# Seven products of quarters in chunks 6 to 10 of the first feed-forward, and the S5 tables and the memory norm moved into chunks 1 to 5

## The chip, the cores and the metric

The kernel runs on one core of a Trainium2 chip. Its time is the device time of one execution in microseconds (us), the median of several runs. All matrices are float32. TensorE (PE) multiplies and transposes into PSUM; VectorE (DVE), ScalarE (ACT) and GpSimd (POOL) work on SBUF, the first two on PSUM too; SyncE (SP) issues most of the DMAs.

## The reference, cut to what matters

```
h = x
h = h + 0.5 * swiglu(rmsnorm(h, g_ffn1), w1_gate, w1_up, w1_down)     # first feed-forward
u = rmsnorm(h, g_mix) @ w_in                                           # mixer: S5 scan and pooling
h = h + concat(rmsnorm(s5(u[:, :1024])), rmsnorm(pool(u[:, 1024:]))) @ w_out
h = h + cross_attention(rmsnorm(h, g_xattn), rmsnorm(mem, g_mem))
h = h + 0.5 * swiglu(rmsnorm(h, g_ffn2), w2_gate, w2_up, w2_down)     # second feed-forward
return rmsnorm(h, g_final)
swiglu(x, g, u, d) = (silu(x @ g) * (x @ u)) @ d
```

There are 256 tokens, the model width is 2048, the hidden width of a feed-forward 5632. The S5 tables (powers of the discretised state matrix, and products of them with B and C) and the norm of the memory depend on no activation, so they can be worked out at any time before the mixer and the attention.

## The kernel before

Each float32 operand is split into a high and a low part (`fp32r`), and a product is three matmuls: high by high, high by low, low by high. A weight tile has 128 x 4 x 512 numbers (1 MB). SyncE loads it into one of three `raw` buffers (pool `wraw`), ScalarE copies a half of it to `whi` (L142), VectorE subtracts that from the half to get `wlo` (L143), and PE uses a half in 12 matmuls of 512 columns: two blocks, two groups of 128 tokens (`lt`), three matmuls (L156 to L158). The activations are the stationary operand, the weights move. A tile is 24 matmuls.

A feed-forward goes over the hidden width in 11 chunks of 512. In a plain chunk the gate needs four weight tiles and the up product four, 192 matmuls in all; `gated` (L274) and `upped` (L285) form the product of the two, `act_tiles` (L289) transposes it (8 matmuls of 128 columns), and four more tiles (96 matmuls) multiply it by the down weights; `add_to_h` (L261) adds the accumulators to `h`. A pass is a group of chunks whose down products are accumulated together.

The first feed-forward (`ffn`, L297) runs plain chunks in the passes `PASSES` of 3, 3, 3 and 2 chunks; the down products of a pass follow its last chunk. The accumulators lie in `psA`, 6 banks, 2 for a gate and 2 for an up product. `begin` (L560) is chunk 0: it loads x, splits it, fills `h` by transposes and takes the gate and up products of a tile pair in turn, with four accumulators open at once. Only behind it does `ffn_norm` (L269) work out the norm of x from the sums of squares that `squares` collects, and `gated` needs its result `hcol`. A generator, `aside` (L544), holds the S5 tables (`s5_tables`, L345) and then the memory norm; `step` (L302) takes a step of it at 5 of 9 tiles, from the seventh on, over the whole feed-forward. Its tiles lie in the pool `pp`.

The second feed-forward is written out of its own (L1020 on). Its passes, `PASSES2`, have two chunks each and one at the end. `psA` has 4 banks for gates and ups and 2 more, `dacc`, for the down products of the pass before, which are taken in steps between the products of the next chunks. Chunks 0 and 1 are plain, chunks 2 to 10 are `seven` (L1100): tokens, inputs and outputs of the upper half of the inputs are taken as quarters, and seven products of 12 matmuls stand for eight; the lower half is plain (`eight`, four tiles). That is 84 + 96 = 180 matmuls in place of 192, for 8 more subtractions of 128 x 1024 (`less`, L1064), and sums of accumulators. `token_sums` (L1083) forms the four sums of token quarters, SH and SL, in two buffers of `wraw`. The halves of weights lie in five pairs of buffers in turn, `pairs[:] = [whl, sw, whl, sw, whl]` (L1079): three in the pool `whl`, two in the pool `sw`. In the first feed-forward there are the three of `whl` alone.

Tile pools are closed and opened in the order of the program; a planner orders the instructions of each engine by program order and by its own costs, and the instructions named in `keep_in_program_order` keep their place.

Of the kernel before, what the change touches and what calls it, by code (L numbers as in the profile page):

```python
# [14 lines left out]
P = 128  # L15
# [8 lines left out]
PASSES2 = ((0, 2), (2, 4), (4, 6), (6, 8), (8, 10), (10, 11))  # L24
PASSES = ((0, 3), (3, 6), (6, 9), (9, 11))
# [29 lines left out]
def block_kernel(ctx: ExitStack, tc: tile.TileContext, xT, memT, wgu1, wd1, w_in, w_glu, w_pool, w_out,  # L55
# [10 lines left out]
    banks = ExitStack()  # L66
    psA = banks.enter_context(tc.tile_pool(name="psA", bufs=6, space=bass.MemoryType.PSUM))
    psB = banks.enter_context(tc.tile_pool(name="psB", bufs=2, space=bass.MemoryType.PSUM))
# [228 lines left out]
    def ffn(fe, wgu, wd, xs, aside=None, begin=None, before=None, after=None):  # L297


        calls = [0]  # L300

        def step():  # L302
            calls[0] += 1
            if aside is not None and calls[0] > 6 and calls[0] * 5 % 9 < 5:
                next(aside, None)

        late = []

        def held(more=None):
            def run(i):  # L310
                if i == 0:
                    while late:
                        late.pop(0)()
                if more is not None:
                    more(i)
                step()
            return run

        for a, b in PASSES:
            acts = []  # L320
            for f in range(a, b):
                if f == 0 and begin is not None:
                    ag, au = begin()
                else:
                    ag, au = tok_unit([cols4(wgu[4 * f:4 * f + 4, 0], i) for i in range(4)], xs, held(before if f == 0 else None)), None
                if f == 0:
                    ffn_norm()
                ss = gated(fe, ag)
                if au is None:
                    au = tok_unit([cols4(wgu[4 * f:4 * f + 4, 1], i) for i in range(4)], xs, held())  # L330
                upped(ss, au)
                late += [lambda ss=ss, t=t: act_tiles(ss, acts, t) for t in range(2)]
            for n in range(ND):
                more = None
                if b == FC and after is not None:
                    more = lambda i, n=n: after(n, i)
                add_to_h(tok_unit([cols4(wd[f, 4 * n:4 * n + 4], 0) for f in range(a, b)], acts, held(more)), n, qcol)
                if b == FC:
                    squares(n)
        if aside is not None:  # L340
            for _ in aside:
                pass

# [199 lines left out]
    with tc.tile_pool(name="pp", bufs=1) as pp, tc.tile_pool(name="fe1", bufs=2) as fe:  # L543
        def aside():  # L544
            yield from s5_tables(pp)
            ss = pp.tile([P, L], F32, name="ssm")
            mt_ = {}
            for k in range(KT + 4):
                if k < KT:
                    mt_[k] = pp.tile([P, L], F32, name="mem", bufs=6)  # L550
                    tc.keep_in_program_order(V.memset(mt_[k][:, :1], 0.0))
                    G.dma_start(out=mt_[k], in_=memT[:, k])
                if k > 3:
                    square_into(ss, mt_[k - 4], k == 4, pin=True)
                if k % 2 == 0:
                    yield
            rnorm(ss, D, rmcol)
            spread(rmcol, Rm)

        def begin():  # L560
# [64 lines left out]
        ffn(fe, wgu1, wd1, xs, aside(), begin,  # L625
            after=lambda n, i: layer_in(xm, n - 1, G_MIX, [xp] * KT) if n > 0 and i == 1 else None)
# [393 lines left out]
    banks.close()  # L1020
    psA = ctx.enter_context(tc.tile_pool(name="psC", bufs=4, space=bass.MemoryType.PSUM))
    psB = ctx.enter_context(tc.tile_pool(name="psD", bufs=2, space=bass.MemoryType.PSUM))
    fe = ctx.enter_context(tc.tile_pool(name="fe2", bufs=2))
    gate_up = lambda f, m: wgu2[4 * f:4 * f + 4, m]
    late = []

    def flush(n=2):
        for _ in range(min(n, len(late))):
            late.pop(0)()

    def finish_chunk(ss, acts):
        late.extend([lambda t=t: act_tiles(ss, acts, t) for t in range(2)])

    def plain(f, acts, before=None):
        def first(i):
            flush()
            if before is not None:
                before(i)

        ag = tok_unit([cols4(gate_up(f, 0), i) for i in range(4)], xf, first)  # L1040
        if f == 0:
            ffn_norm()
        ss = gated(fe, ag, 2)
        upped(ss, tok_unit([cols4(gate_up(f, 1), i) for i in range(4)], xf))
        finish_chunk(ss, acts)

    def down(a, b, acts, accs_of=tok_accs, done=None):

        for n in range(ND):
            accs = accs_of()  # L1050
            for i, f in enumerate(range(a, b)):
                blocks = wtile(cols4(wd2[f, 4 * n:4 * n + 4], 0))
                flush()
                for j, w in enumerate(blocks):
                    tok_block(accs, w, acts[4 * i + j], i + j == 0, f == b - 1 and j == 3)
                if f == b - 1:
                    add_to_h(accs, n, qcol)
                    if done is not None:
                        done(n)
                yield  # L1060

    def less(out, a, b):
        for c in (0, 256):
            V.tensor_tensor(out=out[:, :, c:c + 256], in0=a[:, :, c:c + 256], in1=b[:, :, c:c + 256], op=ALU.subtract)  # L1064

    def product(acc, w, x, first, last):

        acc = acc.rearrange("p (f c) -> p f c", f=4)
        for j, (wh, wl) in enumerate(parts(w)):
            xh, xl = x(j)  # L1070
            T.matmul(acc, xh, wh, start=first and j == 0, stop=False)  # L1071
            T.matmul(acc, xh, wl, start=False, stop=False)  # L1072
            T.matmul(acc, xl, wh, start=False, stop=last and j == 3)  # L1073

    def quarter(k, lt):
        return lambda j: [xf[k + j][:, i * L + lt * P:i * L + (lt + 1) * P] for i in range(2)]

    with tc.tile_pool(name="sw", bufs=1) as sw:
        pairs[:] = [whl, sw, whl, sw, whl]  # L1079
        SH = sw.tile([P, 4, 4, P], F32R, name="SH")  # L1080
        SL = sw.tile([P, 4, 4, P], F32R, name="SL")

        def token_sums():  # L1083

            x = wraw.tile([P, 8, L], F32, name="raw")
            for k in range(8):
                V.tensor_tensor(out=x[:, k], in0=xf[k][:, :L].bitcast(F32), in1=xf[k][:, L:].bitcast(F32), op=ALU.add)
            q = [[x[:, 4 * i:4 * i + 4, lt * P:(lt + 1) * P] for i in range(2)] for lt in range(2)]
            s = wraw.tile([P, 4, 4, P], F32, name="raw")
            for o, a, b, op in ((0, q[1][0], q[1][1], ALU.add), (1, s[:, 0], q[0][0], ALU.subtract),  # L1090
                                (2, q[0][0], q[1][0], ALU.subtract), (3, q[0][1], s[:, 1], ALU.subtract)):
                V.tensor_tensor(out=s[:, o], in0=a, in1=b, op=op)
            for o in (0, 2):
                S.activation(out=SH[:, o:o + 2], in_=s[:, o:o + 2], func=AF.Copy)
                V.tensor_tensor(out=SL[:, o:o + 2], in0=s[:, o:o + 2], in1=SH[:, o:o + 2].bitcast(F32), op=ALU.subtract)

        def tsum(o):
            return lambda j: (SH[:, o, j], SL[:, o, j])

        def seven(f, acts, steps):  # L1100

            g, u = gate_up(f, 0), gate_up(f, 1)
            
            def step():
                flush()
                next(steps, None)


            def load(pool, name, src):
                r = pool.tile([P, 4, 512], F32, name=name)  # L1110
                src(r)
                return r

            tmp = lambda: psB.tile([P, 512], F32, name="psb")
            s1, s5, u2, u3 = (sw.tile([P, 512], F32, name=n) for n in ("s1", "s5", "u2", "u3"))
            t = sw.tile([P, 4, 512], F32, name="t")
            gate, up = ([psA.tile([P, 512], F32, name="acc") for _ in range(2)] for _ in range(2))
            eight = lambda accs, w, i: [tok_block(accs, b, xf[4 * i + j], i == 2 and j == 0, i == 3 and j == 3)
                                        for j, b in enumerate(wtile(cols4(w, i)))]
            r11 = load(wraw, "raw", cols4(g, 0))  # L1120
# [41 lines left out]
        for a, b in PASSES2:  # L1162
            acts = []
            for f in range(a, b):
                if f < 2:
                    plain(f, acts, (lambda i: layer_in(xf, ND - 1, G_FFN2, [xp] * KT) if i == 3 else None) if f == 0 else None)
                    if f == 0:
                        token_sums()
# [129 lines left out]
```

## Time and profile before

| | us |
|---|---|
| median of 3 runs (2132.37 to 2134.86) | 2133.53 |
| the profiled execution | 2133.47 |
| its span, first to last instruction | 2131.7 |
| PE busy / DVE / ACT / POOL | 2094.1 / 1502.4 / 1076.6 / 142.7 |
| mean granted clock of PE | 0.995 |

The page of the profile gives the busy time of each engine, the chain of work that ended last, and the costliest groups of instructions. A line that begins with `L142 ACT` is a group: line of the kernel, engine, operation, output and inputs. In a timeline each line is a start, a duration, an engine, a line and an operation. PE is the weight-streaming engine, PEld its loading of the stationary operand.

### The profile page before, as it was taken

Reading aid. Unit: us, or ns where it says so; the run is one execution under the profiler, and the core shown is the slowest. Engines: PE = TensorE matmul, PEld = TensorE weight load, DVE = VectorE, ACT = ScalarE, POOL = GpSimd, SP = SyncE. Lnnn points to the kernel's source line nnn. Section 1 sums busy time; section 2 is a strip of 40 time slices with the busy share of each in tenths; the row PEclk is TensorE's granted clock in tenths of the full one; section 3 lists DMA queues with packets and bytes.
Section 4 is the critical chain, followed back from the end, with each engine's and each line's share of the span. In section 5 each row is a group of like instructions: output and inputs, shape, how many; then the busy total and the mean of one; then the engine's idle time right before and its main releaser. Section 6 shows DMA issues by size and latency. Waiting matters only on the chain.

```text
span 2131.7 us, 26764 instructions
## 1 busy us (share of the span) xinstructions
PE 2094.1 (98%) x10248; PEld 1730.5 (81%) x10248; DVE 1502.4 (70%) x2021; ACT 1076.6 (51%) x1505; POOL 142.7 (7%) x255
## 2 busy tenths in 40 slices
PE   8999999999999999979999999999999999999997
PEld 7888888888888888867888888888888888888885
DVE  5567766666655667836867755566888888888875
ACT  6543444344444555635665644545555555555543
POOL 0000011111110001850000000000000000000000
PEclk9999999999999999999999999999999999999998
DMA  7756777777766657768544546557565666565542
GB/s 243 209 183 197 206 214 223 218 218 219 229 212 195 226 191 238 252 204 254 197 162 176 202 173 220 195 172 224 177 199 178 195 208 210 180 199 191 178 157 99
DMA packets 202464, 427.58 MB, mean 201 GB/s; under 512 B 17888, under 2 KB 31392, under 8 KB 193248
## 3 DMA queue, kind: packets, MB, share of 16 engines
q1 hardware_dynamic: 180992, 391.75, 58.1%
q0 software_dynamic: 6416, 18.85, 3.0%
q10 hardware_dynamic: 14928, 15.28, 2.3%
q8 instruction: 80, 1.31, 0.2%
q14 instruction: 48, 0.39, 0.1%
HBM read 408.05 MB, written 16.78 MB: 199 GB/s over the span
## 4 chain that ended last, share of the span: by engine, by line
PE 94%; POOL 3%; DMA 1%; DVE 1%; ACT 1%; issue 0%; DVEq 0%; ACTq 0%; SPq 0%
PE acc L158 19%; PE acc L157 19%; PE acc L156 19%; PE acc L120 7%; PE acc L121 4%; PE dacc L156 3%; PE dacc L157 3%; PE dacc L158 3%; PE psb L1072 2%; PE psb L1073 2%; PE psb L1071 2%; PE acc L998 1%; PE acc L999 1%; PE acc L997 1%; PE acc L1072 1%; PE acc L1071 1%
## 5 line engine op out<-in xcount | busy, mean ns | idle before, releaser
L143 DVE TENSOR_TENSOR wlo<-raw,whi 128x1024 fp32r<-128x1024 f32 x522 | 635.9, 1223 | 357.1 <-ACT whi L142 354.9
L142 ACT ACTIVATE whi<-raw 128x1024 fp32r<-128x1024 f32 x522 | 553.0, 1060 | 641.7 <-PE acc L158 461.1
L157 PE MATMUL acc<-wlo,x 128*128 128x512 f32 x1760 | 689.9, 392 | 0.0
L158 PE MATMUL acc<-whi,x 128*128 128x512 f32 x1760 | 687.6, 392 | 0.0
L156 PE MATMUL acc<-whi,x 128*128 128x512 f32 x1760 | 638.5, 393 | 8.2 <-ACT x L191 7.9
L156 PEld LDWEIGHTS acc<-whi,x 128*128 128x128 f32 x1760 | 330.6, 188 | 78.6 <-ACT x L191 7.9
L158 PEld LDWEIGHTS acc<-whi,x 128*128 128x128 f32 x1760 | 330.9, 188 | 70.7 <-issue 1.2
L157 PEld LDWEIGHTS acc<-wlo,x 128*128 128x128 f32 x1760 | 331.0, 188 | 70.0 <-issue 0.6
L120 PE MATMUL acc<-x,whi 128*128 128x512 f32 x848 | 299.7, 399 | 2.4 <-ACT whi L100 2.4
L101 DVE TENSOR_TENSOR wlo<-raw,whi 128x1024 fp32r<-128x1024 f32 (+1 forms) x144 | 172.1, 1199 | 133.6 <-ACT whi L100 133.0
L121 PE MATMUL acc<-x,wlo 128*128 128x256 f32 x848 | 234.9, 283 | 0.9 <-DVE wlo L101 0.8
L100 ACT ACTIVATE whi<-raw 128x1024 fp32r<-128x1024 f32 (+1 forms) x144 | 147.0, 1024 | 163.0 <-PE acc L120 99.3
L120 PEld LDWEIGHTS acc<-x,whi 128*128 128x128 f32 x848 | 158.4, 188 | 40.8 <-ACT whi L100 4.2
L121 PEld LDWEIGHTS acc<-x,wlo 128*128 128x128 f32 x848 | 159.0, 189 | 5.3 <-DVE wlo L101 2.5
L156 PE MATMUL dacc<-whi,x 128*128 128x512 f32 x320 | 124.9, 395 | 1.0 <-DVE h L267 1.0
L158 PE MATMUL dacc<-whi,x 128*128 128x512 f32 x320 | 125.7, 393 | 0.0
L157 PE MATMUL dacc<-wlo,x 128*128 128x512 f32 x320 | 125.4, 392 | 0.0
L142 ACT ACTIVATE whi<-t 128x1024 fp32r<-128x1024 f32 x54 | 57.4, 1062 | 50.4 <-PE acc L158 30.2
L143 DVE TENSOR_TENSOR wlo<-t,whi 128x1024 fp32r<-128x1024 f32 x54 | 65.0, 1224 | 20.5 <-ACT whi L142 19.6
L143 DVE TENSOR_TENSOR wlo<-r,whi 128x1024 fp32r<-128x1024 f32 x54 | 65.9, 1220 | 15.2 <-ACT whi L142 15.2
L142 ACT ACTIVATE whi<-r 128x1024 fp32r<-128x1024 f32 x54 | 56.3, 1059 | 36.6 <-PE acc L158 15.1
L156 PEld LDWEIGHTS dacc<-whi,x 128*128 128x128 f32 x320 | 60.1, 188 | 14.2 <-issue 1.3
(287 smaller groups left out, 2132.2 us busy)
## 6 DMA issues: line engine op xcount, KB each, us to landing
raw<-in_wgu SPq DMA_DIRECT2D x148, 1024.0 KB, 6.1
raw<-in_wd SPq DMA_DIRECT2D x88, 1024.0 KB, 5.3
r<-in_wgu SPq DMA_DIRECT2D x27, 1024.0 KB, 6.1
raw<-in_w_in SPq DMA_DIRECT2D x16, 1024.0 KB, 5.0
raw<-in_w_k SPq DMA_DIRECT2D x16, 1024.0 KB, 5.0
raw<-in_w_out SPq DMA_DIRECT2D x32, 512.0 KB, 5.1
raw<-in_w_q SPq DMA_DIRECT2D x16, 1024.0 KB, 4.8
raw<-in_w_v SPq DMA_DIRECT2D x16, 1024.0 KB, 4.8
```

Source lines behind the costliest of these rows:

```text
L100: S.activation(out=hi[:, :n], in_=r, func=AF.Copy)
L101: V.tensor_tensor(out=lo[:, :n], in0=r, in1=hi[:, :n].bitcast(F32), op=ALU.subtract)
L120: T.matmul(acc, w[0], x, start=first, stop=False)
L121: T.matmul(acc[:, :L], w[1], x[:, :L], start=False, stop=last)
L142: S.activation(out=hi, in_=raw[:, :, c:c + 256], func=AF.Copy)
L143: V.tensor_tensor(out=lo, in0=raw[:, :, c:c + 256], in1=hi.bitcast(F32), op=ALU.subtract)
L156: T.matmul(acc, xh, w[0], start=first, stop=False)
L157: T.matmul(acc, xh, w[1], start=False, stop=False)
L158: T.matmul(acc, xl, w[0], start=False, stop=last)
L1071: T.matmul(acc, xh, wh, start=first and j == 0, stop=False)
L1072: T.matmul(acc, xh, wl, start=False, stop=False)
L1073: T.matmul(acc, xl, wh, start=False, stop=last and j == 3)
```

## The change

`ffn` now serves both feed-forwards, with the passes of two chunks for both and with the chunk from which `seven` is used: 6 in the first, 2 in the second. The first feed-forward therefore has 4 + 2 accumulator banks in place of 6 (`open_banks`), takes its down products between those of the next chunks, and opens the pool `sw` at chunk 6, in the room of `pp`, which must be done by then. The generator `aside` begins with the memory norm, then makes the tables, and takes 1 or 2 steps in turn at each of the 8 gate and up tiles of chunks 1 to 5. `token_sums` is called ahead of chunk 5 (first) and of chunk 1 (second feed-forward). `pairs` has `sw` only from the first chunk with seven products on, which in the second feed-forward is chunk 2, no longer chunk 0. In the last chunk, two steps of the down products are taken at each of four places, where there was one.

```diff
-PASSES = ((0, 3), (3, 6), (6, 9), (9, 11))
+PASSES = ((0, 2), (2, 4), (4, 6), (6, 8), (8, 10), (10, 11))
+SEVEN1 = 6
+SEVEN2 = 2
...
-    psA = banks.enter_context(tc.tile_pool(name="psA", bufs=6, space=bass.MemoryType.PSUM))
+    def open_banks(n):
+        banks.close()
+        return [banks.enter_context(tc.tile_pool(name="ps", bufs=b, space=bass.MemoryType.PSUM)) for b in (n, 2)]
+
+    psA, psB = open_banks(4)
...
+        def steps(slot, slots=4):
+            flush()
+            for _ in range((slot + 1) * todo[1] // slots - slot * todo[1] // slots):
+                next(todo[0], None)
+
+        def plain(f):
+            def ahead(m):
+                def run(i):
+                    if i % 2 == 1 or todo[1] == 0:
+                        steps(2 * m + i // 2)
+                    if before is not None and f == 0 and m == 0:
+                        before(i)
+                    if tick is not None:
+                        tick()
+                return run
...
         for a, b in PASSES:
             acts = []
             for f in range(a, b):
+                if f == seven_from - 1:
+                    SH, SL = (fe.tile([P, 4, 4, P], F32R, name=n, bufs=1) for n in ("SH", "SL"))
+                    token_sums()
+                if f == seven_from:
+                    sw = room()
+                    pairs[:] = [whl, sw, whl, sw, whl]
+                ss = seven(f) if f >= seven_from else plain(f)
...
+            if b < FC:
+                todo[0] = down(wd, a, b, acts, lambda: [psA.tile([P, 512], F32, name="dacc", bufs=2) for _ in range(2)])
+                n = next(y - x for x, y in PASSES if x == b)
+                todo[1] = ND * (b - a) // n
+        pairs[:] = [whl]
+        return down(wd, *PASSES[-1], acts, done=squares if done is None else done)
...
-            yield from s5_tables(pp)
             ss = pp.tile([P, L], F32, name="ssm")
...
             spread(rmcol, Rm)
+            yield from s5_tables(pp)
...
+        def tick():
+            count[0] += 1
+            for _ in range(1 + (count[0] % 2)):
+                next(side, None)
+
+        def room():
+            for _ in side:
+                pass
+            spare.close()
+            return spare.enter_context(tc.tile_pool(name="sw", bufs=1))
+
+        for n, i in ffn(fe, wgu1, wd1, xs, SEVEN1, room, begin, tick=tick):
+            if n > 0 and i == 0:
+                layer_in(xm, n - 1, G_MIX, [xp] * KT)
+        spare.close()
+    psA, psB = open_banks(6)
```

`seven`, `token_sums`, `product`, `less` and `down` are those of the second feed-forward before, moved up.

## Rows read from the trace of the kernel before

**Rows 1.** The page: busy time of the engines, and the chain by engine.
```profile
PE 2094.1 (98%) x10248; PEld 1730.5 (81%) x10248; DVE 1502.4 (70%) x2021; ACT 1076.6 (51%) x1505; POOL 142.7 (7%) x255
...
PE 94%; POOL 3%; DMA 1%; DVE 1%; ACT 1%; issue 0%; DVEq 0%; ACTq 0%; SPq 0%
```

**Rows 2.** Waits of PE: us in total, times, longest.
```profile
PE psb L828 <- DMA big<-big: 12.1, 1, 12.1
...
PE dacc L156 <- DVE h L267: 1.0, 1, 1.0
```

**Rows 3.** Stretches: us, busy (count) of PE, PEld, DVE, ACT, POOL; clock, DMA, GB/s.
```profile
600.00:645.00 45.00, 45.00 (x200) 37.28 (x199) 25.47 (x37) 20.04 (x25) 4.31 (x8) 1.00 0.72 222
1445.00:1490.00 45.00, 45.00 (x201) 36.76 (x200) 30.34 (x31) 20.45 (x24) 0.00 (x0) 1.00 0.71 213
1580.00:1625.00 45.00, 45.00 (x201) 36.73 (x200) 41.05 (x44) 24.02 (x27) 0.00 (x0) 1.00 0.69 211
```

**Rows 4.** Timeline of ScalarE: the tanh that follows each gate, in both feed-forwards.
```profile
80.06 1.37 ACT L279 ACTIVATE th<-acc,hcol 128x512 f32<-128x512 f32 x2 [0.65 <-PE acc L158]
...
124.52 1.37 ACT L279 ACTIVATE th<-acc,hcol 128x512 f32<-128x512 f32 x2 [0.98 <-PE acc L158]
...
1533.92 0.71 ACT L279 ACTIVATE th<-s,hcol 128x512 f32<-128x512 f32 x1
...
2049.82 0.71 ACT L279 ACTIVATE th<-s,hcol 128x512 f32<-128x512 f32 x1
```

**Rows 5.** Timeline of PE: first half of chunk 1, second feed-forward.
```profile
1442.43 0.39 PE L156 MATMUL acc<-whi,x 128*128 128x512 f32 x1
...
1445.23 0.39 PE L156 MATMUL acc<-whi,x 128*128 128x512 f32 x1
```

**Rows 6.** The chain of waits: the eight transposes of a chunk.
```profile
74.82 0.87 PE psb L293 x8
```

**Rows 7.** Groups of instructions, VectorE: the longest operation of the S5 tables.
```profile
L357 DVE TENSOR_TENSOR va<-va,w 128x576 f32<-128x576 f32 x16 | 12.0, 751 | 0.0
```

**Rows 8.** Timelines of PE, VectorE and ScalarE, end of chunk 0.
```profile
57.78 0.48 PE L156 MATMUL acc<-whi,x 128*128 128x512 f32 x1
...
60.84 0.17 DVE L245 TENSOR_REDUCE rv<-ssq 128x2 f32<-128x16 f32 x1 [1.33 <-ACT evq L241]
...
61.89 1.23 DVE L143 TENSOR_TENSOR wlo<-raw,whi 128x1024 fp32r<-128x1024 f32 x1
...
65.94 0.17 DVE L271 TENSOR_SCALAR hcol<-rcol 128x2 f32<-128x2 f32 x1
...
67.20 1.25 ACT L279 ACTIVATE th<-acc,hcol 128x512 f32<-128x512 f32 x2
...
68.47 1.28 DVE L281 SCALAR_TENSOR_TENSOR s<-th,acc 128x512 f32<-128x512 f32 x2
```

**Rows 9.** Stretches behind two idle times of PE.
```profile
8.00:14.00 6.00, 6.00 (x15) 4.71 (x16) 4.01 (x8) 4.25 (x9) 0.00 (x0) 1.00 1.06 382
935.00:939.00 4.00, 3.44 (x51) 3.04 (x52) 0.00 (x0) 0.00 (x0) 0.26 (x1) 0.54 0.65 166
939.00:949.00 10.00, 10.00 (x104) 8.41 (x102) 3.55 (x4) 4.84 (x7) 0.00 (x0) 1.00 0.60 175
```

**Rows 10.** Timelines of VectorE and ScalarE: token sums, second feed-forward.
```profile
1420.49 2.76 DVE L1087 TENSOR_TENSOR raw<-x 128x256 f32<-128x256 f32 x8
...
1426.17 1.29 DVE L1092 TENSOR_TENSOR raw<-raw 128x512 f32<-128x512 f32 x2
...
1432.05 2.35 DVE L1095 TENSOR_TENSOR SL<-raw,SH 128x1024 fp32r<-128x1024 f32 x2
...
1438.76 2.01 ACT L142 ACTIVATE whi<-raw 128x1024 fp32r<-128x1024 f32 x2 [6.66 <-DMA raw<-in_wgu]
```

**Rows 11.** Timelines of ScalarE and VectorE: one half, first feed-forward.
```profile
249.50 1.06 ACT L142 ACTIVATE whi<-raw 128x1024 fp32r<-128x1024 f32 x1 [1.64 <-PE acc L158]
...
250.60 1.23 DVE L143 TENSOR_TENSOR wlo<-raw,whi 128x1024 fp32r<-128x1024 f32 x1 [1.96 <-ACT whi L142]
```

More of the change, by code (lines that the diff above doesn't have):

```diff
@@ L295, in act_tiles @@
             acts.append(split(ap_, pt[:, j]))
[L297 to L317, printed above, removed]
+    late = []
@@ new lines, in flush, with down @@
+    def flush():
+        while late:
+            late.pop(0)()
+    def down(wd, a, b, acts, accs_of=tok_accs, done=None):
+        for n in range(ND):
+            accs = accs_of()
+            for i, f in enumerate(range(a, b)):
+                blocks = wtile(cols4(wd[f, 4 * n:4 * n + 4], 0))
+                flush()
+                for j, w in enumerate(blocks):
+                    tok_block(accs, w, acts[4 * i + j], i + j == 0, f == b - 1 and j == 3)
+                if f == b - 1:
+                    add_to_h(accs, n, qcol)
+                    if done is not None:
+                        done(n)
+                yield n, i
@@ new lines, in less, with product @@
+    def less(out, a, b):
+        for c in (0, 256):
+            V.tensor_tensor(out=out[:, :, c:c + 256], in0=a[:, :, c:c + 256], in1=b[:, :, c:c + 256], op=ALU.subtract)
+    def product(acc, w, x, first, last):
+        acc = acc.rearrange("p (f c) -> p f c", f=4)
+        for j, (wh, wl) in enumerate(parts(w)):
+            xh, xl = x(j)
+            T.matmul(acc, xh, wh, start=first and j == 0, stop=False)
+            T.matmul(acc, xh, wl, start=False, stop=False)
+            T.matmul(acc, xl, wh, start=False, stop=last and j == 3)
@@ L321, in ffn @@
             for f in range(a, b):
[L322 to L341, printed above, removed]
-                pass
+                if f == seven_from - 1:
[5 more added lines that the diff above has]
+                ss = seven(f) if f >= seven_from else plain(f)
+                late.extend([lambda ss=ss, t=t, acts=acts: act_tiles(ss, acts, t) for t in range(2)])
+            for _ in todo[0]:
+                pass
+            if b < FC:
[4 more added lines that the diff above has]
+        return down(wd, *PASSES[-1], acts, done=squares if done is None else done)
     def s5_tables(pp):
@@ L1034, in plain @@
[L1034 to L1073, printed above, removed]
@@ L1176, in block_kernel @@
-    pairs[:] = [whl]
+    spare = ExitStack()
     v, part = (ev.tile([P, 2], F32, name=n, bufs=1) for n in ("v", "part"))
```

202 lines of the change are left out of this document (95 added, 107 removed).

## The prediction

> **What bounds the kernel now.** I read the page first: PE is busy for 98% of the span and is 94% of the chain that ended last [rows 1]. Then the waits of PE: apart from the start, one of 12.1 us in the mixer, and none over a microsecond or so in either feed-forward [rows 2]. Then the stretches: in both feed-forwards PE is busy for 45.00 of 45 us, with VectorE at 25.47 of 45 in a plain stretch of the first and at 41.05 in one with seven products of the second [rows 3]. So the feed-forwards are bound by the number of matmuls and by the pitch at which they follow each other, and an instruction on another engine costs nothing until PE has to wait for it. The same rows hold a second thing: with PE always busy, loading of the stationary operand (PEld, one load for each matmul) takes 37.28 us in the first feed-forward and 36.73 to 36.76 in the second. So 1.4% fewer matmuls go through in the second, in plain chunks as well as in those with seven products.
>
> **The matmuls that go.** A chunk with seven products has 180 gate and up matmuls in place of 192, with 96 down matmuls 276 in place of 288. Five chunks lose 60. What one is worth is read from the tanh behind each gate [rows 4]: 124.52 - 80.06 = 44.46 us are 192 matmuls and the 8 transposes of 0.87 us [rows 6], so 0.2270 us a matmul, and 288 x 0.2270 + 0.87 = 66.25 us a plain chunk. In the second feed-forward (2049.82 - 1533.92) / 8 = 64.49 us a chunk, so 63.62 / 276 = 0.2305 us a matmul. Five chunks: 5 x (66.25 - 64.49) = **-8.8 us**. At 0.2270 it would be 60 x 0.2270 = -13.6. I take -8.8 because the slow matmuls can be placed: the first half of chunk 1 of the second feed-forward is the 17th, by the turn of five a buffer of `sw`, and its 12 matmuls take 1445.23 - 1442.43 = 2.80 us, 0.2333 each [rows 5]; two of five halves at 0.2333 and three at 0.2270 make 0.2295, most of 0.2305. The change gives the first feed-forward the same turn of five. The Trainium skill (SBUF — State Buffer, section "SBUF: two separate sides") says that PE's ports never wait on another engine; nothing in it would make the pool of a weight half matter, and by it the sum would have -13.6 here. The trace disagrees in the second feed-forward, and whether it will in the first is a rival below.
>
> Chunks 0 and 1 of the second feed-forward now use `whl` alone: 384 gate and up matmuls x 0.0035 = **-1.3** (bounds -1.3 and 0). In its last chunk the down steps are no longer taken five in a row behind the product, where a `dacc` waited 1.0 us for its addition [rows 2]: **-1.0** (or 0).
>
> **The accumulators of chunk 0.** This is a wait that the trace doesn't have. `begin` holds four accumulators, and the gate of chunk 1 needs two more. With six banks it starts at 57.78, while the gate of chunk 0 is still being read until 68.47 + 1.28 = 69.75 [rows 8], since tanh waits for `hcol`, the last link of the norm of x. With four banks (the two `dacc` banks are another tile) PE must wait for that reading, and everything that PE has left is queued behind. No down product is ready then. The norm itself gets faster: its reduce stands at 60.84, `hcol` ends at 66.1, with two `wlo` of 1.23 us between that belong to chunk 1 and now can't be made, as all three weight halves are full. That puts `hcol` at 63.6. From the start of tanh to the first free accumulator the trace has 67.20 to 69.1 with another `wlo` of about 0.6 us in the way: 1.4 us. PE starts at about 65.1, **+7.3 us**. If nothing gets faster it is 69.1 - 57.8 = 11.3; less than 6.5 I don't see. Then the clock: behind an idle PE the rows show matmuls at the 1.2 GHz level. At the start of the kernel 15 in 6.00 us, which at 0.227 take 3.4, a loss of 2.6; after the 12.1 us in the mixer a granted clock of 0.54 over 935 to 939, with PE busy 3.44 of these 4 us, a loss of 1.7, and 1.00 from 939 [rows 9]. A wait of 7.3 us lies between: **+2.2** (0 if the clock stays, 3.7 if as long as the wait).
>
> **The token sums.** They hold two of three `raw` buffers, so the next weight tile is loaded late. In the second feed-forward ScalarE idled 6.66 us for it, until 1438.76; `wlo` was there at 1438.76 + 1.06 + 1.23 = 1441.05, and PE came to it at 1442.43 [rows 5, 10]: 1.4 us to spare. That was with five halves in turn. The buffers of the sums come free when earlier tiles have been split (the sums start at 1420.49 and 1426.17, SL at 1432.05), and with three halves a tile is split two halves later against PE, 2 x 12 x 0.2270 = 5.4 us. 5.4 - 1.4 = 4.0 late; the 8 transposes, 0.87, can fill some: **+3.0** (0 to 4.0). In the first feed-forward the same, ahead of chunk 5, while VectorE also makes tables: **+3.5** (0 to 6).
>
> **What moves.** The tables and the memory norm keep every instruction. Their matmuls and transposes cost PE the same in chunk 2 as in chunk 8. One load of 1 MB on SP, 16 memory loads and 72 stores on POOL move with them; POOL is busy 7% [rows 1] and SP has loads two tiles ahead, so I put 0 on the queues. On VectorE a table chunk has 12 operations of at most 0.751 us [rows 7], 9.0 us, in four steps, and 12 steps go into a chunk of some 67 us: 27 us more than the plain 25.47 x 67 / 45 = 38, 65 of 67 by durations. Consecutive operations overlap a little, and 41.05 of 45 in the second feed-forward made PE wait for nothing [rows 3]. The cover is the lead of a half: `whi` starts when PE has freed the third half before it, 249.50, `wlo` ends at 251.83 [rows 11], and PE comes 5.4 us behind the start, so 3.1 us of lead. One operation of 0.75 ahead of a `wlo` is hidden; a whole step of six (4.5 us) would show 1.4. I put **+0.5**, with 16 such steps, 22 us, as the far bound. 56 steps at 1.5 a tile are done at the 37th of 40 tiles, some five tiles (27 us) before chunk 6, so `sw` opens in time; SP's later weights would queue behind a late `r12` load, 0 in the sum. The end of the first feed-forward, four tiles with additions, squares and splits in place of eight, and the change of banks there: **+1.5** (0 to 3), from the 1.0 us that the same form cost in the second [rows 2]. More additions to `h` (passes of two) lie under PE.
>
> **Sum.** -8.8 - 1.3 - 1.0 + 7.3 + 2.2 + 3.0 + 3.5 + 1.5 + 0.5 = +6.9 on the profiled execution's 2133.47 (span 2131.7), which is within 0.1 of the median: **2140.4 us**, slower by 0.3%. 0.2%, 4.3 us, is about what a measurement of this kernel can tell from no change.
>
> **The rivals.**
> (a) The loads cover the token sums: a buffer comes free early enough that PE never sees them. Place: ahead of chunks 5 and 1; price -6.5, 2133.9, not slower. It decides once two halves less of lead are worth under 1.4 us. For it: 1.4 us to spare and no wait in the trace; against: 5.4 us less lead. 0.17.
> (b) The matmuls of chunks 6 to 10 run at 0.2270, wherever the halves lie (what the skill's page would have): -13.6 for -8.8, 2135.6. Against: plain chunks of the second feed-forward are as slow as its others [rows 3]. 0.08.
> (c) PE doesn't wait at chunk 1, because the planner finishes the norm of x earlier: -9.5, 2130.9. Against: it needs all of x, and its last squares are behind the last transposes of chunk 0 [rows 8]. 0.08; with (a) it is faster, 2124.
> (d) VectorE becomes the bound in chunks 3 to 5: half of the 22 us, 2151. 0.07.
> (e) The sum as it stands, own range 2136 to 2146: 0.60.
>
> **Numbers.** Slower: nearly all of (e), (d) and a little of (a) and (b), 0.66. Within 0.2%: most of (a) and (b), some of (c) and a little of (e), 0.25. Faster: (c) with (a) or (b), 0.09. The range that leaves out (c) and most of (d) is 2133 to 2148.
>
> **What would show it.** Right: an idle PE of 6 to 8 us at about 58 us, ended by L281, and a pitch of 0.43 behind it; a wait of PE of some 3 us for `whi` ahead of chunk 5 and of chunk 1 of the second feed-forward; tanh to tanh 64.5 us in chunks 7 to 10. Wrong: no wait at chunk 1, or 62.8 to 63.5 us from tanh to tanh, or VectorE without idle time in chunks 3 to 5 and PE waiting for `wlo` again and again.

## The result, and the profile of the changed kernel

| us | before | changed |
|---|---|---|
| median (runs) | 2134.2 (4, 2132.37 to 2135.27) | 2149.65 (4, 2149.14 to 2152.95) |
| the profiled execution, its span | 2133.47, 2131.7 | 2152.95, 2151.1 |
| PE busy, matmuls and transposes | 2094.1, 10248 | 2094.3, 10188 |

The changed kernel is slower: ratio 1.0071, 95% interval 1.0058 to 1.0083, 15.4 us. The direction was foreseen, the size was not: 6.9 us were forecast, and 2149.65 lies above the range. The profiled execution is the slowest of the four by 3.2 us, so what follows is about 19.4 us of span, some 3 of which the other three runs don't have.

The page, which answers to [rows 1]:

```profile
PE 2094.3 (97%) x10188; PEld 1721.4 (80%) x10188; DVE 1619.0 (75%) x2161; ACT 1115.4 (52%) x1547; POOL 142.4 (7%) x255
...
PE 88%; DMA 3%; POOL 3%; DVE 3%; ACT 1%; issue 1%; SPq 0%; DVEq 0%; ACTq 0%; POOLq 0%
```

Sixty matmuls are gone and PE is busy as long as before, and the chain runs over other engines for 12% of the span where it was 6%. So there are two questions: where PE waits, and why its work takes longer. The waits of PE between 14 and 772 us, that is in the first feed-forward (total, times, longest); none of these was there before [rows 2]:

```profile
PE acc L161 <- DVE s L286: 7.0, 1, 7.0
PE dacc L162 <- DVE wlo L148: 2.5, 1, 2.5
PE acc L161 <- ACT whi L147: 1.9, 1, 1.9
PE dacc L161 <- DVE h L272: 0.7, 1, 0.7
PE psb L298 <- ACT s L407: 0.7, 1, 0.7
PE acc L162 <- DVE wlo L148: 0.4, 1, 0.4
```

They sum to 13.2 us and lie at three places: chunk 1, the tile behind the token sums, and the start of chunk 6.

**Chunk 1**, timelines of PE and ScalarE, answering to [rows 8] and [rows 4]:

```profile
63.09 1.27 ACT L284 ACTIVATE th<-acc,hcol 128x512 f32<-128x512 f32 x2 [2.81 <-DVE hcol L276]
...
64.55 0.80 PE L161 MATMUL acc<-whi,x 128*128 128x512 f32 x1 [7.05 <-DVE s L286]
...
89.55 1.37 ACT L284 ACTIVATE th<-acc,hcol 128x512 f32<-128x512 f32 x2 [0.36 <-PE acc L163]
```

PE stands still for 7.05 us until the gate of chunk 0 has been read, and chunk 1's tanh comes at 89.55 in place of 80.06: 9.5 us. The stretches behind it show the other 2.4 (us; busy of PE, PEld, DVE, ACT, POOL; clock; DMA; GB/s), as [rows 9] do for two idle times of before: 13 matmuls in 5.5 us at a granted clock of 0.50, the 1.2 GHz level.

```profile
64.50:70.00 5.50, 5.45 (x13) 4.34 (x14) 1.92 (x3) 0.00 (x0) 0.00 (x0) 0.50 0.00 0
70.00:75.00 5.00, 5.00 (x27) 4.20 (x26) 1.18 (x3) 1.62 (x4) 0.00 (x0) 0.97 0.00 0
```

**The token sums**, timelines of SP's queue and PE, answering to [rows 10] for the first feed-forward:

```profile
299.27 0.37 SPq L154 DMA_DIRECT2D raw<-in_wd  x1
318.41 2.96 SPq L154 DMA_DIRECT2D raw<-in_wgu  x2
...
325.85 0.83 PE L161 MATMUL acc<-whi,x 128*128 128x512 f32 x2 [1.94 <-ACT whi L147]
```

SP issues no load for 19 us. The three `raw` buffers go round in turn: the sums take two, so the next tile gets the buffer of the tile that is just being split (e9 below tests this). Behind the wait the granted clock was 0.76 over 323 to 330 us, which cost another 1.7.

**Chunk 6**, timelines of POOL, SP, ScalarE and PE. The last store of the tables lands at 388.8; only then is their room free, and SP's load of `r12` (tile `r`), which stands ahead of other loads, is issued:

```profile
380.46 2.32 POOL L656 DMA_DIRECT2D Kd<-kr  x4 [4.70 <-ACT kr L653]
...
388.84 0.37 SPq L154 DMA_DIRECT2D r<-in_wgu  x1
389.31 0.45 SPq L154 DMA_DIRECT2D raw<-in_wd  x1
...
388.94 2.96 ACT L147 ACTIVATE whi<-raw 128x1024 fp32r<-128x1024 f32 x3 [3.18 <-DMA Kd<-kr]
...
398.74 0.50 PE L162 MATMUL dacc<-wlo,x 128*128 128x512 f32 x1 [2.52 <-DVE wlo L148]
...
405.03 0.66 PE L298 MATMUL psb<-ident,s 128*128 128x128 f32 x4 [0.69 <-ACT s L407]
```

In the chain of waits between 378 and 410 us the store and the load that waits for it stand one behind the other:

```profile
382.20 6.55 DMA Kd<-kr
...
388.84 6.33 DMA r<-in_wgu
```

**The sevens** themselves and the mixer's start, timelines of ScalarE and PE. From tanh to tanh 64.61 us, near the 64.49 of the second feed-forward before [rows 4]; a plain chunk took 66.25. PE's first matmul of the mixer comes at 773.84 against 761.44 in the trace of before:

```profile
449.14 0.71 ACT L284 ACTIVATE th<-s,hcol 128x512 f32<-128x512 f32 x1
...
513.75 0.71 ACT L284 ACTIVATE th<-s,hcol 128x512 f32<-128x512 f32 x1
...
773.84 0.47 PE L125 MATMUL acc<-x,whi 128*128 128x512 f32 x1 [0.94 <-DVE h L272]
```

The 30 us around it, of which PE is busy 26.99 (before, 758 to 788: 28.95); 0.94 of the difference is the wait in the line above:

```profile
770.00:800.00 30.00, 26.99 (x152) 22.26 (x152) 20.03 (x43) 16.77 (x35) 0.52 (x1) 1.00 0.38 129
```

So the loss is 12.4 us where the mixer starts, 18.8 at the last matmul of the mixer's and attention's projections (1222.20 against 1203.37), and 19.4 at the end.

### The profile page after: what moved, and what is told of

Same layout as the page of the kernel before. It is cut to its first block, busy times and chain, and to the rows that moved or that the text cites. A ratio compares the mean times of both kernels' runs of the same rounds, so it can differ in the third digit from the quotient of the medians.

```text
span 2151.1 us, 26841 instructions
## 1 busy us (share of the span) xinstructions
PE 2094.3 (97%) x10188; PEld 1721.4 (80%) x10188; DVE 1619.0 (75%) x2161; ACT 1115.4 (52%) x1547; POOL 142.4 (7%) x255
## 4 chain that ended last, share of the span: by engine, by line
PE 88%; DMA 3%; POOL 3%; DVE 3%; ACT 1%; issue 1%; SPq 0%; DVEq 0%; ACTq 0%; POOLq 0%
PE acc L162 13%; PE acc L161 13%; PE acc L163 13%; PE acc L125 7%; PE dacc L161 7%; PE dacc L162 7%; PE dacc L163 7%; PE acc L126 3%; PE psb L333 2%; PE psb L332 2%; PE psb L334 2%; PE acc L333 2%; PE acc L332 2%; PE acc L334 2%; PE acc L1139 1%; PE acc L1140 1%
## 5 line engine op out<-in xcount | busy, mean ns | idle before, releaser
L148 DVE TENSOR_TENSOR wlo<-raw,whi 128x1024 fp32r<-128x1024 f32 x492 | 596.5, 1221 | 180.8 <-ACT whi L147 176.8
L162 PE MATMUL acc<-wlo,x 128*128 128x512 f32 x1280 | 504.0, 394 | 0.8 <-DVE wlo L148 0.8
L163 PE MATMUL acc<-whi,x 128*128 128x512 f32 x1280 | 499.5, 393 | 0.0
L161 PE MATMUL acc<-whi,x 128*128 128x512 f32 x1280 | 464.5, 395 | 19.3 <-ACT x L196 8.0
L161 PEld LDWEIGHTS acc<-whi,x 128*128 128x128 f32 x1280 | 241.3, 189 | 72.8 <-ACT x L196 8.0
L162 PEld LDWEIGHTS acc<-wlo,x 128*128 128x128 f32 x1280 | 242.0, 189 | 54.6 <-DVE wlo L148 2.0
L163 PEld LDWEIGHTS acc<-whi,x 128*128 128x128 f32 x1280 | 241.8, 189 | 52.1
L162 PE MATMUL dacc<-wlo,x 128*128 128x512 f32 x640 | 251.9, 394 | 2.5 <-DVE wlo L148 2.5
L163 PE MATMUL dacc<-whi,x 128*128 128x512 f32 x640 | 250.6, 394 | 0.0
L161 PE MATMUL dacc<-whi,x 128*128 128x512 f32 x640 | 246.1, 395 | 0.7 <-DVE h L272 0.7
L148 DVE TENSOR_TENSOR wlo<-t,whi 128x1024 fp32r<-128x1024 f32 x84 | 101.8, 1223 | 58.2 <-ACT whi L147 58.0
L162 PEld LDWEIGHTS dacc<-wlo,x 128*128 128x128 f32 x640 | 120.2, 188 | 29.9 <-DVE wlo L148 2.9
L161 PEld LDWEIGHTS dacc<-whi,x 128*128 128x128 f32 x640 | 119.6, 188 | 27.0 <-DVE h L272 0.9
L163 PEld LDWEIGHTS dacc<-whi,x 128*128 128x128 f32 x640 | 120.2, 188 | 26.0
```

What stands on the lines that cost most here:

```text
L148: V.tensor_tensor(out=lo, in0=raw[:, :, c:c + 256], in1=hi.bitcast(F32), op=ALU.subtract)
L161: T.matmul(acc, xh, w[0], start=first, stop=False)
L162: T.matmul(acc, xh, w[1], start=False, stop=False)
L163: T.matmul(acc, xl, w[0], start=False, stop=last)
```

## The experiments

All medians are beside 2134 to 2136 us for the kernel before on the same chip, and the changed kernel's 2149.65. "Mixer" is PE's first matmul of the mixer in the profiled execution, which tells of the first feed-forward alone.

| run | edit of the changed kernel | median (range), us | mixer, us |
|---|---|---|---|
| e1 | six accumulators for chunks 0 and 1 | 2142.93 (2141.5 to 2146.4) | 762.74 |
| e2 | two steps of the tables a tile | 2153.55 (2152.6 to 2154.8) | 775.40 |
| e3 | last pass has two chunks | 2146.85 (2144.3 to 2152.5) | 769.14 |
| e4 | no sevens in the first feed-forward | 2150.52 (2149.2 to 2152.7) | 772.53 |
| e5 | `sw` moved by 320 bytes | 2139.19 (2135.4 to 2142.0) | 768.39 |
| e6 | token sums in two rounds | 2151.86 (2148.2 to 2155.3) | 772.69 |
| e7 | e6 and e2 | 2149.58 (2145.6 to 2155.3) | 771.33 |
| e8 | e7, e1 and e3 | 2143.49 (2140.8 to 2146.9) | 766.06 |
| e9 | token sums in place, one buffer | 2146.68 (2145.3 to 2147.8) | 769.90 |
| e10 | e1, e5, e9, 1.75 steps a tile, other passes | 2126.86 (2123.6 to 2128.4) | 761.08 |
| e11, e12 | `sw` moved by 64, by 128 bytes | 2140.11, 2147.81 (one run each) | 767.59, 772.16 |
| e13 | kernel before, `sw` moved by 320 bytes | 2124.98 (2122.7 to 2125.4) | 760.63 |
| e14 | e10 with the passes of the change | 2119.98 (2119.1 to 2121.7) | 752.14 |
| e15 | e10, pass of one chunk among plain ones | 2123.12 (2118.9 to 2125.1) | 754.81 |

**e1, the accumulators.**

```diff
-  ag, au = tok_unit([cols4(gate_up(f, 0), i) for i in range(4)], xs, ahead(0)), None
+  ag, au = tok_unit([cols4(gate_up(f, 0), i) for i in range(4)], xs, ahead(0),
+                    [psA.tile([P, 512], F32, name="dacc", bufs=2) for _ in range(2)] if f == 1 and begin is not None else None), None
```

> One edit: the gate of chunk 1 of the first feed-forward takes its two accumulators from the dacc banks, which nothing uses before chunk 2, so that chunk 0 and chunk 1 have six as before the change. Theory (each wait of the changed kernel has its own price, and they add): the 7.3 us wait of PE at 57 us and the slow clock behind it, 2.2 us by the distance of the first tanh of chunk 1 from that of before (89.55 against 80.06), go: 2149.6 - 9.5 = 2140.1 us. Rival (the time was hidden slack: tables, stores and weight loads that now have 9.5 us less until chunk 6 are late by that much there): the waits at chunk 6 grow from 4.3 to some 10 us or more, and the time falls by less than 4, to 2146 or more.

The wait is gone, chunk 1's tanh stands at 79.10 and the mixer starts 11.1 us earlier. By medians it is 6.7 us, against 9.5 of the theory: the wait was a cost, but its size is shown by single executions alone, and where the other 2.8 went is not shown. The waits at chunk 6 did not grow (2.4, 0.7 and 0.8 us), so the rival falls.

**e2, e7: the room for chunk 6.**

```diff
-            for _ in range(1 + (count[0] % 2)):
+            for _ in range(2):
```

> One edit: two steps of the memory norm and the tables a tile in place of one and a half, so that the 56 steps end at tile 28 of 40 and not at 37. Theory: the waits of PE at the start of chunk 6 (2.9, 1.1 and 1.0 us at 395 to 406 us, 4.3 over the pitch) come from the last store of the tables, which lands at 388.7 us, just when chunk 6 wants the room; with the tables done 9 tiles earlier they go, and nothing else grows: 2145.3 us. Rival (VectorE is what binds chunks 2 to 5): VectorE is at 33.7 of 38 us at its densest, one third more tables a tile puts it at the whole of the time, PE waits for wlo there, and the time grows by 3 us or more, to 2153.

The waits at chunk 6 went, but the wait behind the token sums grew, and the clock fell behind it (0.72 over 331 to 337 us): 3.9 us slower. The row of PE in e2 that answers to the one at 325.85, then SP's queue, then one link of the chain of waits:

```profile
335.95 1.22 PE L161 MATMUL acc<-whi,x 128*128 128x512 f32 x2 [4.63 <-ACT whi L147]
```

```profile
319.28 1.47 SPq L154 DMA_DIRECT2D r<-in_wgu  x3
322.88 2.64 SPq L154 DMA_DIRECT2D raw<-in_wgu  x2
```

```profile
322.88 11.87 DMA raw<-in_wgu
```

The rival's size was nearly right and its mechanism wrong: there is no run of waits for `wlo`, and VectorE is busy for only 3.79 of 6 us from 325 to 331. The room for chunk 6 now opens so early that SP issues three loads of 1 MB into it (`r`) just ahead of the weight tile that PE needs next. That tile takes 11.87 us to land, against some 6.3 in the changed kernel (issued at 318.41, split from 324.74). Whether a fuller VectorE adds to it is not shown. e7, with e6's sums, lost 1.8 us there and had a single wait of 0.3 at chunk 6, yet its median is that of the changed kernel:

> Two edits: the token sums in one raw buffer at a time, and two steps of the tables a tile. Theory (the late room at chunk 6 costs 4.3 us, and what two steps a tile lost alone was the token sums meeting a busier VectorE): the waits at 395 to 406 us go and no wait at 331 us comes back: 2143.4 - 4.3 = 2139.1 us. Rival (VectorE itself is too full with two steps a tile): short waits for wlo all through chunks 2 to 4, and a time no better than that of the sums alone.

Neither theory nor rival gives that by itself; its runs spread over 10 us, so I draw nothing from the total.

**e6, e9: the token sums.** e6 makes them in two rounds, each in half of one buffer:

```diff
-            x = wraw.tile([P, 8, L], F32, name="raw")
...
-            s = wraw.tile([P, 4, 4, P], F32, name="raw")
+            for j in (0, 2):
+                r = wraw.tile([P, 8, L], F32, name="raw")
+                x, s = r[:, :4], r[:, 4:].rearrange("p o (b c) -> p o b c", b=2)
...
```

> One edit: the token sums, in both feed-forwards, are made in two rounds of half the blocks, each in one buffer of raw in place of two, so two of the three stay free for weight tiles. Theory (the sums hold the buffers, and the weight tile is loaded late): the waits of PE at 323 us (1.94 and 0.42, and some 1.9 of slow clock behind them) and at 1461 and 1502 us (1.5 and 0.4) go: 2149.6 - 6.2 = 2143.4 us. Rival (VectorE's queue is late, because the sums stand in it ahead of the halves): the waits stay, and the time with them, 2149.6 within 1.5.

A miss: PE waited 3.42 us there, longer than before. I had counted how many buffers are held at a time, and what matters is how many turns are taken: two rounds are two turns, and SP still issued nothing from 298 to 318 us. e9 takes one turn:

```diff
-            s = wraw.tile([P, 4, 4, P], F32, name="raw")
-            for o, a, b, op in ((0, q[1][0], q[1][1], ALU.add), (1, s[:, 0], q[0][0], ALU.subtract),
...
+            for out, a, b, op in ((q[1][1], q[1][0], q[1][1], ALU.add), (q[1][0], q[0][0], q[1][0], ALU.subtract),
+                                  (q[0][0], q[1][1], q[0][0], ALU.subtract), (q[0][1], q[0][1], q[0][0], ALU.subtract)):
+                V.tensor_tensor(out=out, in0=a, in1=b, op=op)
...
```

> One edit: the token sums, in both feed-forwards, are made in place in a single buffer of raw. The two rounds of e6 still took two buffers in turn, one after the other, so the next weight tile still had to wait for the buffer of the tile just ahead of it (SP issued nothing between 299 and 318 us, in the changed kernel as in e6). With one buffer taken, the next tile has a buffer that is free already. Theory: the waits at 323 us (1.94, 0.42, and some 1.9 of slow clock) and at 1461 and 1502 us (1.5 and 0.4) go or shrink to a third: 2149.6 - 5 = 2144.6 us. Rival (VectorE's lateness): SP loads on time, but whi and wlo of the next halves wait behind the sums on ScalarE and VectorE, and PE's waits stay: 2149.6 within 1.5.

SP's queue in e9, beside that of the changed kernel above:

```profile
298.78 0.37 SPq L154 DMA_DIRECT2D raw<-in_wd  x1
311.83 6.45 SPq L154 DMA_DIRECT2D raw<-in_wgu  x2
323.98 0.37 SPq L154 DMA_DIRECT2D raw<-in_wd  x1
```

The load comes 6.6 us earlier, PE has no wait over 0.3 us there, the mixer starts 3.9 us earlier, and the median falls by 3.0. The buffers were the cause; the edit of e6 was the wrong test of it. The gain is not the whole price of the sums: behind the wait at chunk 6, 2.6 us as before, the granted clock now fell (0.66 over 393 to 398 us, where the changed kernel has 1.00). In the second feed-forward a wait of 1.1 us stays.

**e3, e15: the end of the first feed-forward.** e3 replaces the passes there by (0, 1), (1, 3), (3, 5), (5, 7), (7, 9), (9, 11).

> One edit: the passes of the first feed-forward are (0,1), (1,3), (3,5), (5,7), (7,9), (9,11) in place of (0,2) to (8,10), (10,11), so its last down products take two tiles for each quarter of h, as before the change, and additions, squares, transposes and splits have twice the time. Theory: from the start of chunk 1's th to the 56th matmul of the mixer's first product the changed kernel loses 0.9 us to the wait for h and 2.9 us in the mixer's first products, 3.9 in all, and these go: 2145.8 us. Rival (the loss there is from the change of banks or the late weight loads at it, not from the spacing): no change, 2149.6 within 1.5.

In e3 PE is busy 28.07 of the 30 us around the mixer's start (765 to 795 us), where the changed kernel has 26.99 and the kernel before 28.95: 1.1 of 2.0 us come back there. The median fell by 2.8, but its runs spread over 8 us. In e15 against e14 the mixer's start is better by the profile (28.08 of 30, 751 to 781, against 27.02, 748 to 778) and the first feed-forward ends later, and the medians say 3.1 slower. All the traces together say more than one pair. From the mixer's first matmul to the last one of the mixer's and attention's projections it takes 446.0 to 452.6 us in the eleven kernels whose first feed-forward ends with a pass of one chunk, 443.0 to 445.8 in the four that end with two (e3, e8, e10, e15), and 441.9 and 444.9 in the kernel before and e13. So a last pass of one chunk costs some 4 us there by the means, one execution of each kernel; what moving the one-chunk pass elsewhere costs in the first feed-forward has to be set against it, and the sum stays open.

**e4, what the sevens earn as changed.** `SEVEN1 = 12`.

> One edit: chunks 6 to 10 of the first feed-forward are plain, so there are no token sums, no room and no seven products in it; the order of the tables, the passes and the four accumulators stay as changed. Theory: the seven products give 5 x (66.25 - 64.6) = 8.2 us, and the token sums (4.3 us at 323 us) and the start of chunk 6 (4.3) take 8.6 from it, so this runs in the same time as the changed kernel, 2149.2. Rival (the seven products are worth their whole 60 matmuls at 0.2267, 13.6, and the rest of the loss lies elsewhere, as in the denser chunks 1 to 5): 2149.6 + 13.6 - 8.6 = 2154.6 us or more.

As the theory had it: 2150.5. In the changed kernel the seven products of the first feed-forward give 8.2 us, and their sums and their room take it back.

**e5, e11, e12, e13: the slow matmuls.** By the allocation of the compiled programs, which no profile shows, the weight halves of `whl` begin 352 bytes past a multiple of 512 in a partition, that is 96 past one of 128, and those of `sw` 32 past one of either, in the kernel before too. The sizes of the tiles in the two kernels, added up in the order of the pools and each rounded up to 32 bytes, give the same distances between `whl` and `sw`.

```diff
+        sw = spare.enter_context(tc.tile_pool(name="sw", bufs=1))
+        V.memset(sw.tile([P, 80], F32, name="gap"), 0.0)
```

(80 numbers in e5 and e13, 16 in e11, 32 in e12.)

> One edit: 320 bytes a partition stand unused at the front of the pool sw, in both feed-forwards, so that its weight halves start 352 bytes past a multiple of 512, as those of whl do, and not 32 bytes past one. Theory (the slow matmuls, 0.233 us against 0.227, come from where the moving half starts): from tanh to tanh a chunk with seven products takes 276 x 0.2268 + 0.87 = 63.5 us in place of 64.6, and fourteen such chunks in all make 15 us: 2134 us. Rival (the pitch is slow for another reason: how full ScalarE and VectorE are in such chunks, or what else PE reads): tanh to tanh stays at 64.6 and the time at 2149.6, within 1.5.

> One edit: 64 bytes at the front of sw, so that its halves start 96 bytes past a multiple of 512 and of 256, as far past a multiple of 256 as those of whl (352 = 256 + 96). Theory (what counts is the place within 256 bytes or less): tanh to tanh 63.7 us, as with 320 bytes. Rival (it counts within 512 bytes or more, or any move does something else): another value, 64.6 if nothing changes.

> One edit: 128 bytes at the front of sw, so that its halves start 160 bytes past a multiple of 512, which is 32 past one of 128, as in the changed kernel (32), while those of whl are 96 past one of 128. Theory (the place within 128 bytes counts): tanh to tanh 64.6 us, as without the move. Rival (any place but the old one is good, or the place within 256 or 512 counts): 63.7 or another value.

The tanh of e5 in chunks 6 and 7 (447.68 and 511.36), of e11 (510.59, then 574.28), of e12 (512.89, then 577.24) and of e13 in the second feed-forward, each fence one kernel:

```profile
447.68 0.71 ACT L284 ACTIVATE th<-s,hcol 128x512 f32<-128x512 f32 x1
511.36 0.71 ACT L284 ACTIVATE th<-s,hcol 128x512 f32<-128x512 f32 x1
```

```profile
510.59 0.71 ACT L284 ACTIVATE th<-s,hcol 128x512 f32<-128x512 f32 x1
...
574.28 0.71 ACT L284 ACTIVATE th<-s,hcol 128x512 f32<-128x512 f32 x1
```

```profile
512.89 0.71 ACT L284 ACTIVATE th<-s,hcol 128x512 f32<-128x512 f32 x1
...
577.24 0.71 ACT L284 ACTIVATE th<-s,hcol 128x512 f32<-128x512 f32 x1
```

```profile
1534.07 0.71 ACT L279 ACTIVATE th<-s,hcol 128x512 f32<-128x512 f32 x1
...
1597.61 0.71 ACT L279 ACTIVATE th<-s,hcol 128x512 f32<-128x512 f32 x1
```

64.61 us became 63.68 with 320 and 63.69 with 64 bytes, but 64.35 with 128. So of the four places tried for `sw` the two that are 96 past a multiple of 128 are fast and the two that are 32 past one are slow, a little less so at 160 past 512 than at 32 past it. The edit moves the other tiles of `sw` too, but in the changed kernel PE reads nothing but the halves out of it. Whether a multiple of 128 is the right measure, and what lies behind it, is open. 14 chunks at 0.93 are 13.0 us, and e5's median fell by 10.5.

> The kernel before the change with one edit: 320 bytes at the front of its pool sw, so that its weight halves start 352 past a multiple of 512 and not 32 past one. Theory (the pitch comes from the place of the moving half, and the changed kernel's first feed-forward gets nothing else from its seven products): tanh to tanh in the second feed-forward falls from 64.49 to 63.6 us, nine chunks and the two plain ones that use sw in turn give 9 x 0.9 + 1.3 = 9.4 us: 2134.9 - 9.4 = 2125.5 us, the same as all five edits on the changed kernel (2126.9), which would mean that the seven products in the first feed-forward earn nothing even with the waits mended. Rival (the place matters only where the change has put sw): 64.49 and 2134.9 as before.

The kernel before gains the same way: 63.54 for 64.49 from tanh to tanh, 2124.98, ratio 0.9947 (0.9934 to 0.9961). In its plain chunk 1 of the second feed-forward, where only the halves of `sw` are in use, 39 matmuls in a row now go at 0.2267 us, with no half at the 0.2333 of [rows 5]:

```profile
1439.89 0.39 PE L156 MATMUL acc<-whi,x 128*128 128x512 f32 x1
...
1448.73 0.39 PE L156 MATMUL acc<-whi,x 128*128 128x512 f32 x1
```

That is the yardstick for the rest: a version of the change is worth something only if it beats 2125.

**e8, e10, e14: together.**

> Four edits: six accumulators for chunks 0 and 1, the token sums in one raw buffer at a time, two steps of the tables a tile, and passes that end with two chunks, (9,11). Theory (the four losses are separate and add): 2139.1 less the 6.7 and 2.8 us that the first and the last gave alone: 2129.6 us, faster than before the change. Rival (the waits take each other's place, since the tables, the stores and the loads have less time as PE gets faster): 2136 us or more.

2143.5, the rival's side. The first pass of one chunk was a mistake of mine: its down products use `dacc` while chunk 1's gate stands there, and waits of 1.1, 0.5 and 0.5 us came at 81 to 92 us. Six more, 3.9 us in all, lie between 205 and 329 us, for weight halves; what causes them was not tested. e10 has the sums of e9, `range(1 + (count[0] % 4 > 0))` steps a tile, and its pass of one chunk as (8, 9):

> Five edits: six accumulators for chunks 0 and 1, token sums in place, seven steps of the tables in four tiles (56 in 32), passes (0,2), (2,4), (4,6), (6,8), (8,9), (9,11) in the first feed-forward, and the pool sw moved by 320 bytes. Theory (the losses add): 2149.6 - 6.7 (six) - 10.4 (offset) - 2.8 (passes) - 5 (sums) = 2124.7 us, and some 2 less if the room opens in time for chunk 6: faster than before by 10 us. Rival (waits take each other's place, as in the four edits together, which gained 6.2 of 16): 2149.6 - 6.2 - 10.4 = 2133 us, no faster than before.

2126.9, between the two, nearer to the theory's 2124.7. Its longest waits of the first feed-forward lie in that one-chunk pass: 2.13 and 1.20 us at 660 and 669, with the clock at 0.91 over 655 to 675.

> All edits of e10 but the passes, which are those of the change. Theory: the pass of one chunk in the middle of the seven products cost e10 some 4 us (waits of 2.1 and 1.2 us at 658 to 667 us and a slow clock behind them), and the pass of one chunk at the end costs 3.9 at the mixer's start, so the two are even: 2127 us. Rival (the end costs more, as e3 alone gained 2.8): 2130 us.

> As e10, with the passes (0,2), (2,4), (4,5), (5,7), (7,9), (9,11): the pass of one chunk lies in the plain chunks and the last one has two. Theory (waits can be taken away one by one): neither the waits at 658 us nor those at the mixer's start, and fewer down products beside the token sums and the start of chunk 6: 2126.9 - 4 = 2123 us. Rival (VectorE and the loads in chunk 4 then have eight down steps beside the tables, and PE waits there instead): 2127 us.

e14 is the best: 2119.98, ratio 0.9928 (0.9915 to 0.994), 5.0 us under e13. The one wait of PE that its trace lists from 14 to 750 us, against the six above:

```profile
PE acc L162 <- DVE wlo L148: 0.2, 1, 0.2
```

and the mixer's first matmul, in PE's timeline:

```profile
752.14 0.47 PE L125 MATMUL acc<-x,whi 128*128 128x512 f32 x1 [0.91 <-DVE h L272]
```

## Why the prediction was right in sign and wrong in size

| term | forecast | measured |
|---|---|---|
| seven products, five chunks | -8.8 | 5 x (66.25 - 64.61) = -8.2 |
| wait at chunk 1 | +7.3 | +7.05 |
| clock behind it | +2.2 | 9.5 - 7.05 = +2.4 |
| token sums, first feed-forward | +3.5 | +3.9 (e9, mixer); in the trace 1.9 and 0.4 of waits, 1.7 of clock |
| `sw` opens in time | 0 | +3.9 (2.52, 0.69, 0.71 us of waits) |
| end and banks | +1.5 | +0.9 at the mixer's first matmul, some 1.0 behind it |
| second feed-forward (-1.3, -1.0, +3.0) | +0.7 | 19.4 - 18.8 = +0.6 |
| mixer and attention | 0 | 448.4 - 441.9 = +6.5, with the 1.0 of the row on the end |
| VectorE in the chunks with tables | +0.5 | 0: no wait of PE in chunks 1 to 5 but those above |

**The step that failed** is "56 steps at 1.5 a tile are done at the 37th of 40 tiles, some five tiles (27 us) before chunk 6, so `sw` opens in time". I counted when the steps are issued, not when their last reader is done: the last table goes through VectorE, PE, ScalarE and POOL's four stores, which land at 388.8, and SP asks for `r12` ahead of chunk 6 at that same moment. The text named what is behind it ("SP's later weights would queue behind a late `r12` load") and put 0 on it; it cost 3.9. With it the sum is 2144.3, inside the range; it alone does not make 2149.65.

A second term at nothing has no reason given at all: behind "the change of banks" the sum has no mixer and no attention, and there the profiled execution lost 6.5 us, more than at `sw`.

**The rest.** I count 9.5 - 8.2 + 3.9 + 3.9 + 0.9 = 10.0 of the 12.4 us at the mixer's start; 2.4 I can't place. Behind it the mixer and attention took 448.4 us to the last projection against 441.9. About 1.0 of that is the start of the mixer (26.99 busy of 30 against 28.95, less the 0.94 counted above). PE's waits for loads of the tables (tile `tab`) are more, three lines of the changed kernel and the one of before:

```profile
PE psb L875 <- DMA tab<-WTd: 1.9, 2, 1.4
PE psb L967 <- DMA tab<-Kd: 0.8, 1, 0.8
PE psb L969 <- DMA tab<-Vd: 0.6, 1, 0.6
```

```profile
PE psb L826 <- DMA tab<-Kd: 0.3, 1, 0.3
```

The wait for `WTd`, 0.5 to 2.0 us, stands in all fifteen traces with the first feed-forward as changed or mended, and in neither of the two with that of before; so it comes with the change, though nothing here shows why those loads land later. The rest is in part what single executions vary by. e13, which changes nothing ahead of the second feed-forward, took 1205.50 - 760.63 = 444.9 us there, 2.9 more than before. Of that, 1.0 us is the granted clock behind the wait of 12 us (0.74 over 935.3 to 945.3, against 0.84 of before over 935.5 to 945.5) and 0.8 a longer wait for `Kd` (1.1 us). The changed kernel has a clock of 0.76 over 953 to 963. So part of the 6.5 comes with the change, and part need not. The ledger reaches 19.4 and the median 15.4 because the profiled run is the slowest.

Two agreements in the table are of sums and not of terms. In the second feed-forward the waits behind the token sums were 1.5 and 0.4 us where +3.0 stood, and each chunk with seven products took 64.61 us for 64.49, which was not foreseen. And the +2.2 for the clock used a stretch of [rows 9] whose granted clock is listed as 1.00: that PE ran slowly there is read from its pitch alone.

**The rivals.** (a) falls: PE saw the sums in both feed-forwards (1.9 and 1.5 us). (b) falls as put: the pitch was slow in chunks 6 to 10 as forecast. But its core was nearer to the truth than my reason against it. I blamed the pool of `sw`; it was its place, and with it moved the matmuls of those chunks run at (63.69 - 0.87) / 276 = 0.2276. The rule of the Trainium skill that I weighed (SBUF — State Buffer, "SBUF: two separate sides") speaks of engines waiting on each other's ports and does not bear on it. The same page's section "Operand start alignment" lets an operand start at any multiple of its element size and says of this "legality, not speed"; the runs here show the speed. (c) falls: PE waited. (d) falls: in the densest stretch VectorE is at 33.69 of 38 us (282 to 320) with PE at 38.00.

**Did the change do what it is for?** Not as made (e4). With its waits mended and `sw` moved, yes: the first feed-forward ends 8.5 us earlier than that of the kernel before with `sw` moved (752.14 against 760.63), and 5.0 us are left at the end.

## What to carry to other kernels

When space is handed from one stage to the next, date the handover by the landing of the last store that reads it, not by the last step issued, and look at what is queued behind the first load into it: too late, it holds up the loads behind it (3.9 us here), and too early, it stands in front of a load that is needed sooner (e2). In a pool whose buffers go round, a temporary costs turns, not bytes: count how many tiles later the next load can start. And before counting instructions out of a loop bound by one engine, ask why two of its equal instructions differ in pace: here 3% on two of five weight halves were worth more than the change.

## What was not expected of the hardware

A matmul with a moving operand of 128x512 in four runs of 512 bytes goes at about 0.2270 us [rows 4] from halves that start 96 bytes past a multiple of 128 and at about 0.2333 from halves 32 past one [rows 5]; moving the pool by 64 or 320 bytes gave 0.93 us a chunk of 276 matmuls, moving it by 128 gave 0.26. Nothing here tells why.

Equal idle times of PE were not followed by the same loss. Behind 7.05 us the changed kernel ran 13 matmuls in 64.5 to 70.0 us, at a granted clock of 0.50; e3, behind the same 7.05 us, had 17 in that stretch, with a clock of 0.69:

```profile
64.50:70.00 5.50, 5.15 (x17) 4.17 (x18) 2.22 (x4) 0.16 (x1) 0.00 (x0) 0.69 0.00 0
```

So the same wait has cost different sums in two kernels; what decides it stays open.
